# Two mixture-of-experts stages of a two-block kernel: float32r gathers and a smaller weight ring in the first, another order of the first expert's steps in the second

## The chip, the core and the metric

The kernel runs as one program on one core of a Trainium2 chip. The metric is the device time of one execution in microseconds (us). PE is TensorE, which multiplies matrices into PSUM banks (128 partitions x 512 f32 values). DVE (VectorE) and ACT (ScalarE) do elementwise work and carry results from PSUM to SBUF. SP issues the DMA transfers that bring weights from HBM.

## The reference

Two transformer-like blocks run one after the other on 256 tokens of width 1024, all in f32. Each has a token mixer and then a mixture of 32 experts. Only the mixtures matter here. The first picks two of eight experts within the best of four groups; the second picks four of 32 and has biases and a clipped activation:

```python
# first: eid = the two best experts of the best group, w = their weights; E = 32
def expert_block(args):                       # w_gate, w_up: 1024 x 256, w_down: 256 x 1024
    xb, e = args
    return (jax.nn.silu(xb @ w_gate[e]) * (xb @ w_up[e])) @ w_down[e]
# second: top_e = the four best experts, top_w = softmax of their logits
def expert_block(args):                       # w_gu: 1024 x 2048, w_dn: 1024 x 1024
    xe, e = args
    gu = xe @ w_gu[e] + b_gu[e]
    x_glu = jnp.minimum(gu[:, :D_FF], SWIGLU_LIMIT)
    x_lin = jnp.clip(gu[:, D_FF:], -SWIGLU_LIMIT, SWIGLU_LIMIT)
    act = (x_lin + 1) * (x_glu * jax.nn.sigmoid(SWIGLU_ALPHA * x_glu))
    return act @ w_dn[e] + b_dn[e]
# both: every token's results are summed with their weights
```

## The kernel before

**The weight ring.** Nearly all time after the first third of the kernel goes with 2 MB pieces of weights. The class `Ring` (lines 98 to 145) loads them in one fixed order through SP's queue (line 132). A piece is loaded into whichever buffer comes free next, so its transfer waits until the last matmul on the piece that lay there before, and every later piece queues behind it. In the first mixture the ring has four buffers of `ringp`, one more of the same pool under the tag `x`, NR1 = 3 of `ringq`, and one of `ringt` that serves until the first context product: nine buffers, then eight. In the second mixture it has seven.

**The first mixture** (lines 1575 to 1885) takes the 32 experts in eight quads of four, with 32 slots an expert. For quad q, `gather1` makes a 0/1 matrix `Sm` (token against slot) times the tokens' `rstd`, and multiplies it with `x1` on PE (line 1645) into the transposed inputs `xT`; `Sw` holds the same with the tokens' weights and goes through a transpose to `sT`. `up1` (line 1670) multiplies four pieces of gate and up weights, `act1` applies silu, `turn1` transposes, `down1` (line 1697) multiplies two pieces of down weights and adds into `acc` through `sT` (line 1706, the scatter). Slots above 32 are extra work under a branch that reads `nx1`; the trace shows it taken in quads 0 and 7. In quad q the gather of quad q+1 stands between `up1` and `turn1`. Ahead of quads 2, 3 and 4 stand three products of the context (lines 691 and 695), which belong to the second block and use ring pieces too. In quad 0, `weights1` (lines 1578 to 1586) and `extra_blocks1` (to line 1597, which makes `nx1`) run on DVE beside `up1`.

**The second mixture** (lines 2320 to 2840) starts with expert 0, whose weights (`gu` 0 and `dn` 0) are loaded early. `gather2_0` gathers its 64 slots (line 2508) and calls three steps: `compare` and `by_tokens`, which rank the experts by their number of tokens and open the ring for the rest, and `first2`, which issues `up2` (line 2566). Then `rest_by_rank` prepares weights, slots and biases (lines 2443 and 2451 pick the biases on PE) of the experts in ranked order, `gather2` gathers the next two items (line 2531, in float32r from `xh` and `xl`, where `xh` is the rounded value and `xl` the rest), and `down2` (line 2657) finishes expert 0. Items of four slim experts follow with `up2s` (line 2600) and `down2s` (line 2632).

A scheduler moves instructions within an engine's stream, so the order of the code is only roughly that of the engines.

Of the kernel before, what the change touches and what calls it, by code (L numbers as in the profile page):

```python
# [25 lines left out]
NR1 = 3  # L26
# [131 lines left out]
def _body(tc, nc, a, off, es, stop, dump):  # L158
# [11 lines left out]
    def trps():  # L170
        return ps("tr", 2)
# [1453 lines left out]

    def gather1(q, slots, tag, sT=None, between=None):

        Sm = pw1.tile([P, 2, 4, 32], F32, tag="Sm", name="Sm")
        Sw = pw1.tile([P, 2, 4, 32], F32, tag="Sw", name="Sw")
# [6 lines left out]
        xT = pw1.tile([P, 8, P], F32, tag="xT" + tag, name="xT")  # L1639
        for c2 in range(2):  # L1640
            pt = mmps() if tag else ps("sc", 2)
            for cc in range(4):
                c = 4 * c2 + cc
                for n in range(2):
                    PE.matmul(pt[:, P * cc:P * cc + P], xv1[:, n, c, :], Sm[:, n].rearrange("p e s -> p (e s)"),  # L1645
                              start=(n == 0), stop=(n == 1))
            for cc in range(4):
                c = 4 * c2 + cc
                if cc % 2:
                    S.activation(xT[:, c], pt[:, P * cc:P * cc + P], AF.Identity, scale=A2[:, c:c + 1], bias=sh2[:, c])  # L1650
                else:
                    V.tensor_scalar(xT[:, c], pt[:, P * cc:P * cc + P], A2[:, c:c + 1], sh2[:, c], op0=ALU.mult, op1=ALU.add)
        if between is not None:
            between(xT)
            for n in range(2):
                V.tensor_tensor(Sw[:, n], Sw[:, n], bcast(W1[:, n, e4, None], [P, 4, 32]), op=ALU.mult)
        pt = trps()
        for n in range(2):
            PE.transpose(pt[:, P * n:P * n + P], Sw[:, n].rearrange("p e s -> p (e s)"), ident)
        if sT is None:  # L1660
            sT = pw1.tile([P, 2, P], F32, tag="sT", bufs=2, name="sT")
        S.copy(sT, pt[:, :T].rearrange("p (c s) -> p c s", c=2))
        return xT, sT
# [12 lines left out]
    def act1(pg, tag):  # L1676
        act = pw1.tile([P, 256], F32, tag="act" + tag, name="act")
# [36 lines left out]
    def first1(xT):  # L1714
        pg.append(up1(0, xT, ""))
        weights1()
        extra_blocks1()

    nxt = gather1(0, iota[:, 0:32], "", between=first1)
# [112 lines left out]
    for q in range(8):  # L1832
# [17 lines left out]
        xT, sT = nxt  # L1850
# [11 lines left out]
        act = act1(up1(q, xT, "", True) if q else pg[0], "")  # L1862
        if q == 0:
# [558 lines left out]
    def rest_by_rank():  # L2422
        for n in range(2):
            chosen(n, ordr, M2)
        cnt = slots_of(M2, posm2)
        V.tensor_tensor(key, cnt, cap2, op=ALU.subtract)
        weights2(ordr)
        V.tensor_reduce(key[0:1, 0:1], key[0:1], axis=AX.X, op=ALU.max)
        V.tensor_scalar(over2, key[0:1, 0:1], 0.0, None, op0=ALU.max)

# [50 lines left out]
    def back2(Sw, w):  # L2481

        pt = trps()
        for n in range(2):
            PE.transpose(pt[:w, P * n:P * n + P], Sw[:, n, 0:w], ident)
        wc = pw2.tile([P, 1], F32, tag="wc2", bufs=3, name="wc2")
# [5 lines left out]
    def gather2_0(steps):  # L2492
# [22 lines left out]
        return xT, back2(Sw, 64)  # L2515
# [40 lines left out]
    def up2(r, xT, release=True):  # L2556
# [4 lines left out]
        for c in list(range(8)) + [-1] * (r == 0):  # L2561
            w = None if c < 0 else ring.get(("gu", r, c // 2)).rearrange("p (c f) -> p c f", c=2)[:, c % 2]
            for i in range(2):
                for j in range(2):
                    q, o = 4 * r + 2 * i + j, 1024 * i + 512 * j
                    PE.matmul(pg[i][64 * j:64 * j + 64, :], bcast(ident[:, q:q + 1], [P, 64]) if c < 0 else xT[:, c, :],  # L2566
                              bgu if c < 0 else w[:, o:o + 512], start=(r == 0 and c == 0), stop=(c == (7 if r else -1)),
                              tile_position=(0, 64 * j))
# [186 lines left out]
    xT, back = gather2_0((compare, by_tokens, first2))  # L2755
    ordered.close()
    rest_by_rank()
    r2.close()

# [105 lines left out]
```

## Time and profile before

| | before |
|---|---|
| median of three runs | 2023.31 us (2017.72 to 2023.66) |
| profiled execution | 2020.87 us, its span 2019.1 us |
| mean granted TensorE clock | 0.930 of full speed |
| PE busy | 1728.3 us, 86% of the span |
| DVE, ACT busy | 859.4 us (43%), 545.9 us (27%) |
| weight transfers through SP's queue | 628.04 MB, 79.9% of 16 DMA engines' span |

The span is the time from the first to the last instruction; the execution is 1.8 us longer. Busy shares are means over stages that have different limits, so the rows further down are by stage. A granted clock of 1.0 is TensorE's upper level (2.4 GHz), 0.5 its lower one (1.2 GHz).

### The profile page before, as it was taken

How to read it: one execution, taken by the hardware profiler on the slowest of the kernel's cores; microseconds unless marked ns; L12 is line 12 of the kernel's file. 1: busy time of each engine (PE TensorE's matmuls, PEld its weight loads, DVE VectorE, ACT ScalarE, POOL GpSimd, SP SyncE). 2: the span in 40 equal slices, each digit the busy share in tenths (PEclk: the TensorE clock that was granted, in tenths of full speed). 3: DMA queues.
4: the chain of work that ended last, by engine and by line, in shares of the span. 5: the costliest groups of instructions: out<-in, count | busy, mean ns of one | idle time of the engine just before them, and what ended most of it. 6: DMA issues, size and time to landing. Idle time of an engine off the chain costs nothing. (4 is left out here: it accounts for less than half of the span.)

```text
span 2019.1 us, 25531 instructions
## 1 busy us (share of the span) xinstructions
PE 1728.3 (86%) x10043; PEld 956.1 (47%) x10043; DVE 859.4 (43%) x1832; ACT 545.9 (27%) x1184; POOL 257.6 (13%) x232
## 2 busy tenths in 40 slices
PE   5899888989898878789999699886899988999855
PEld 2767667865554538578854133322233333333211
DVE  6998888553112248986644022211122222122112
ACT  4442566322011135566422011110021111111001
POOL 2576322200000005520100000000000000000000
PEclk8898899989999998899979799998899999999986
DMA  8624337976899986742457999999999999899996
GB/s 261 238 95 159 124 135 230 303 270 240 303 364 399 394 275 223 253 126 89 167 210 319 420 419 420 420 422 423 415 424 420 419 423 420 338 421 419 425 420 250
DMA packets 172666, 630.82 MB, mean 312 GB/s; under 512 B 25424, under 2 KB 32016, under 8 KB 152048
## 3 DMA queue, kind: packets, MB, share of 16 engines
q1 hardware_dynamic: 172112, 628.04, 79.9%
q8 instruction: 89, 1.46, 0.3%
q10 hardware_dynamic: 288, 0.52, 0.1%
q0 software_dynamic: 128, 0.39, 0.1%
q14 instruction: 49, 0.40, 0.1%
HBM read 627.88 MB, written 1.05 MB: 311 GB/s over the span
## 5 line engine op out<-in xcount | busy, mean ns | idle before, releaser
L2566 PE MATMUL mm<-w,xT 128*64 128x512 f32 x1472 | 332.0, 605 | 0.0
L2566 PEld LDWEIGHTS mm<-w,xT 128*64 128x64 f32 x1472 | 103.4, 139 | 205.2 <-issue 199.9
L2657 PE MATMUL o<-w,aT 128*64 128x512 f32 x640 | 149.6, 603 | 3.0 <-DMA w<-in_w_dn 3.0
L2600 PE MATMUL mm<-w,xT 128*32 128x512 f32 x768 | 106.6, 686 | 39.5 <-DMA w<-in_w_gu 39.5
L2575 DVE TENSOR_SCALAR g<-mm 128x512 f32<-128x512 f32 x23 | 15.9, 691 | 262.6 <-PE mm L2566 262.6
L2834 POOL TENSOR_TENSOR fin<-acc,fin 128x512 f32<-128x512 f32 x1 | 1.3, 1272 | 978.3 <-DVE acc L2832 978.3
L722 DVE TENSOR_TENSOR lo<-w,hi 128x512 fp32r<-128x512 f32 x126 | 102.1, 823 | 26.5 <-ACT hi L721 24.6
L709 PE MATMUL mm<-hTh,scratch 128*128 128x256 f32 x392 | 93.4, 315 | 9.6 <-DVE scratch L722 9.6
L721 ACT CAST hi<-w 128x512 fp32r<-128x512 f32 x126 | 76.7, 620 | 56.6 <-PE mm L709 50.0
L2632 PE MATMUL o<-w,aT 128*32 128x512 f32 x384 | 70.9, 780 | 23.0 <-DMA w<-in_w_dn 21.1
L2577 ACT ACTIVATE s<-g 128x512 f32<-128x512 f32 x23 | 14.5, 632 | 274.4 <-DVE g L2575 274.4
L2657 PEld LDWEIGHTS o<-w,aT 128*64 128x64 f32 x640 | 44.8, 138 | 87.3 <-issue 79.8
L709 PEld LDWEIGHTS mm<-hTh,scratch 128*128 128x128 f32 x392 | 71.6, 208 | 20.4 <-DVE scratch L722 9.2
L2672 DVE SCALAR_TENSOR_TENSOR yl<-yy,wc,yh 128x512 fp32r<-128x512 f32 (+1 forms) x30 | 21.4, 749 | 134.2 <-ACT yh L2671 134.0
L1670 PE MATMUL mm<-w,xT 128*32 128x512 f32 x640 | 72.0, 594 | 7.4 <-DVEq L1856 2.7
L2600 PEld LDWEIGHTS mm<-w,xT 128*32 128x32 f32 x768 | 23.1, 117 | 108.2 <-DMA w<-in_w_gu 62.1
L709 PE MATMUL mm<-hT3h,lo 128*128 128x256 f32 x192 | 61.4, 320 | 8.5 <-DVE lo L722 5.9
L2687 DVE TENSOR_TENSOR acc<-acc,sc 128x512 f32<-128x512 f32 x56 | 37.0, 685 | 68.3 <-PE sc L2679 68.3
L2662 ACT COPY yy<-o 64x512 f32<-64x512 f32 x40 | 23.2, 580 | 157.0 <-PE o L2657 156.6
L1645 PEld LDWEIGHTS sc<-Sm,x 128*128 128x128 f32 x256 | 61.6, 335 | 6.6 <-issue 5.0
L709 PE MATMUL mm<-scratch 128*128 128x256 f32 x216 | 64.7, 299 | 0.0
L1645 PE MATMUL sc<-Sm,x 128*128 128x128 f32 x256 | 63.2, 409 | 1.3 <-DVE Sm L1636 1.2
(706 smaller groups left out, 3462.2 us busy)
## 6 DMA issues: line engine op xcount, KB each, us to landing
w<-in_w_gu SPq DMA_DIRECT2D x128, 2048.0 KB, 19.9
w<-in_w_dn SPq DMA_DIRECT2D x63, 2048.0 KB, 23.0
w<-in_w_in SPq DMA_DIRECT2D x20, 2048.0 KB, 9.5
w<-in_moe_w_gate SPq DMA_DIRECT2D x32, 1024.0 KB, 10.8
w<-in_moe_w_up SPq DMA_DIRECT2D x32, 1024.0 KB, 12.8
w<-in_moe_w_down SPq DMA_DIRECT2D x32, 1024.0 KB, 13.8
w<-in_ada_w SPq DMA_DIRECT2D x12, 2048.0 KB, 9.7
w<-in_w_mod SPq DMA_DIRECT2D x12, 2048.0 KB, 8.8
```

What stands on the lines that cost most here:

```text
L709: PE.matmul(out, x, y, start=start and i == 0, stop=stop and i == 2)
L721: S.copy(hi, src)
L722: return parts, lambda: V.tensor_tensor(lo, src, hi.bitcast(F32), op=ALU.subtract)
L1645: PE.matmul(pt[:, P * cc:P * cc + P], xv1[:, n, c, :], Sm[:, n].rearrange("p e s -> p (e s)"), start=(n == 0), stop=(n == 1))
L1670: PE.matmul(pg[32 * j:32 * j + 32, :].rearrange("p (j f) -> p j f", j=2), xT[:, c, 32 * j:32 * j + 32], w[:, c % 2], start=(c == 0), stop= ...
L2566: PE.matmul(pg[i][64 * j:64 * j + 64, :], bcast(ident[:, q:q + 1], [P, 64]) if c < 0 else xT[:, c, :], bgu if c < 0 else w[:, o:o + 512], ...
L2600: PE.matmul(pg[32 * t:32 * t + 32, :], xT[:, c, :], w[:, 512 * ij:512 * ij + 512], start=False, stop=(c == 7), tile_position=(0, 32 * t))
L2632: PE.matmul(pd[32 * t:32 * t + 32, :], aT[:, f % 4, 2 * (1 - e) + f // 4, :], w[:, 512 * j:512 * j + 512], start=False, stop=(f == 7), til ...
L2657: PE.matmul(pd[64 * j:64 * j + 64, :], aT[:, f % 4, f // 4, :], w[:, 512 * j:512 * j + 512], start=False, stop=(f == 7), tile_position=(0, ...
L2662: S.copy(y[:, 512 * j:512 * j + 512], pd[64 * j:64 * j + 64, :])
L2672: V.scalar_tensor_tensor(yl[:, o], y[:, o], back[1], yh[:, o].bitcast(F32), op0=ALU.mult, op1=ALU.subtract)
L2687: V.tensor_tensor(o, o, pc, op=ALU.add)
```

## The change

In the first mixture the gathers of quads 1 to 7 are made two quads at a time in float32r: `normalised1` splits the normalised tokens into `xh1` and `xl1` (two instructions on ACT and two on DVE, 128 x 1024 each), and `gather1s` multiplies both with one `Sms` of 256 slots, in quads 0 (for 1 and 2), 2 (for 3 and 4), 4 (for 5 and 6) and 6 (for 7 alone, given twice). Quad 0's own gather and those of the extra slots stay as they were. NR1 becomes 2, so the ring has eight buffers and later seven. In the second mixture `gather2_0` uses two banks with `by_tokens` between their halves, `up2` of expert 0 begins with its bias rows and no longer ends with them, ACT's table for the sigmoid is loaded ahead, and expert 0's `down2` is written ahead of the picking of biases and of `gather2`.

```diff
-NR1 = 3
+NR1 = 2
...
+    def normalised1():
+        for n in range(2):
+            S.activation(xh1[:, n], xv1[:, n], AF.Identity, scale=rstd2[:, n:n + 1])
+            V.scalar_tensor_tensor(xl1[:, n], xv1[:, n], rstd2[:, n:n + 1], xh1[:, n].bitcast(F32), op0=ALU.mult, op1=ALU.subtract)
+
+    def gather1s(qs):
...
+        for c0 in range(0, 8, 2):
+            pt = ps("sc", 2)
+            for c in range(2):
+                for n in range(2):
+                    for x in (xl1, xh1):
+                        PE.matmul(pt[:, T * c:T * c + T], x[:, n, c0 + c, :], Sm[:, n], start=(n == 0 and x is xl1), stop=(n == 1 and x is xh1))
...
     def first1(xT):
         pg.append(up1(0, xT, ""))
+        normalised1()
         weights1()
         extra_blocks1()
...
         if q == 0:
+            turn1(act, aT)
             extras()
             ring.done(4)
-        if q < 7:
-            nxt = gather1(q + 1, iota[:, 0:32], "")
-        aT = pw1.tile([P, 2, P], F32, tag="aT", name="aT")
-        turn1(act, aT)
+        if q % 2 == 0:
+            _, backs1 = gather1s((q + 1, min(q + 2, 7)))
+        if q:
+            turn1(act, aT)
+        if q % 2 == 0:
+            quads = backs1()
         if q < 7:
             down1(q, aT, sT, q == 0, "")
...
-        pt = ps("sc", 2)
+        pts = [ps("sc", 2) for _ in range(2)]
+        for h in range(2):
+            for c in range(4):
+                for n in range(2):
+                    PE.matmul(pts[h][:, 64 * c:64 * c + 64], xv[:, n, 4 * h + c, :], Sm[:, n, 0:64], start=(n == 0), stop=(n == 1))
+            if h == 0:
+                steps[1]()
         for c in range(8):
-            for n in range(2):
-                PE.matmul(pt[:, 64 * c:64 * c + 64], xv[:, n, c, :], Sm[:, n, 0:64], start=(n == 0), stop=(n == 1))
-        steps[1]()
-        for c in range(8):
-            modulated(xT[:, c], pt[:, 64 * c:64 * c + 64], c)
+            modulated(xT[:, c], pts[c // 4][:, 64 * (c % 4):64 * (c % 4) + 64], c)
...
-        for c in list(range(8)) + [-1] * (r == 0):
+        for c in [-1] * (r == 0) + list(range(8)):
...
+        S.activation(warm, warm, AF.Sigmoid)
...
+    pt0 = turned2(Sw0, 64, ps("sc", 2))
     l = act2(pg)
+    slots_by_rank()
+    pd0 = bias2(0, xps())
+    aT0 = turn2(l, pw2.tile([P, 512], F32, tag="g2", name="aT0"))
+    back = back2(Sw0, 64, pt0)
+    down2(0, pd0, aT0, y)
+    ordered.close()
+    biases_by_rank()
+    r2.close()
     cur = gather2(pairs2[0])
-    down2(0, bias2(0, xps()), turn2(l, pw2.tile([P, 512], F32, tag="g2", name="aT0")), y)
```

What this does to the engines' order shows at three places. PE's stream in quad 1 of the first mixture, before: the four pieces of `up1`, the gather of quad 2 (L1645), the transposes of `Sw` and of `act`, then `down1`.

```order
L1670 MATMUL mm<-w_4158,xT 32x512 x8
L1670 MATMUL mm<-w_4161,xT 32x512 x8
L1670 MATMUL mm<-w_4287,xT 32x512 x8
L1670 MATMUL mm<-w_4384,xT 32x512 x8
L1645 MATMUL sc<-Sm,x_68 128x128 x16
L1659 MATMUL tr<-C,Sw 128x128 x2
L1686 MATMUL tr<-C,act 128x128 x2
L1697 MATMUL mm<-w_4387,aT 32x512 x2
L1697 MATMUL mm<-w_4390,aT 32x512 x2
```

The same place now:

```order
L1718 MATMUL mm<-w_4158,xTs 32x512 x8
L1718 MATMUL mm<-w_4290,xTs 32x512 x8
L1718 MATMUL mm<-w_4392,xTs 32x512 x8
L1718 MATMUL mm<-w_4395,xTs 32x512 x8
L1734 MATMUL tr<-C,act 128x128 x2
L1745 MATMUL mm<-w_4398,aT 32x512 x2
L1745 MATMUL mm<-w_4401,aT 32x512 x2
```

In the odd quads nothing stands between `up1` and `down1` but the transpose of `act`; in quads 0, 2, 4 and 6 there are 32 matmuls of 128 x 256 (L1649) and two pairs of transposes.

DVE's stream in quad 0, at the end of quad 0's own gather, before: `xT` is evicted and `weights1` begins.

```order
L1652 TENSOR_SCALAR xT<-sc,A_134,sh_132 128x128 x4
L1578 TENSOR_SCALAR gsc_4088<-t_4085 128x1
L1580 TENSOR_TENSOR gsc_4088<-t8b_4097 128x1
L1582 SCALAR_TENSOR_TENSOR gsc_4088<-gsc_4088 128x1
L1583 RECIPROCAL gsc_4088<-gsc_4088 128x1
```

The same place now:

```order
L1700 TENSOR_SCALAR xT<-sc,A_134,sh_132 128x128 x4
L1633 SCALAR_TENSOR_TENSOR xl_4171<-x_68,rstd_3796,xh_4170 128x1024 x2
L1578 TENSOR_SCALAR gsc_4088<-t_4085 128x1
L1580 TENSOR_TENSOR gsc_4088<-t8b_4097 128x1
L1582 SCALAR_TENSOR_TENSOR gsc_4088<-gsc_4088 128x1
```

The two `xl1` instructions stand ahead of all of `weights1`; ACT's two `xh1` stand likewise ahead of its part of `weights1`.

PE's stream in the second mixture, before, from the last piece of expert 0's `up2` on: bias rows, transposes of `Sw`, counts (L1489 to L1492), the picked biases and the next gather.

```order
L2566 MATMUL mm<-w_9264,xT_9518 64x512 x8
L2566 MATMUL mm<-bgu,C 64x512 x4
L2485 MATMUL tr<-C,Sw_9507 64x128 x2
L1489 MATMUL tr<-M_9456,C 128x32
L1490 MATMUL tr<-M_9456,C 128x64
L1491 MATMUL tr<-M_9456,C 128x32
L1492 MATMUL tr<-M_9456,C 128x32
L2443 MATMUL tr<-bgu,pick 128x512
L2554 MATMUL mm<-bgl,sel 128x512
L2451 MATMUL tr<-bdn,pick 128x512
L2531 MATMUL sc<-Sm_9675,xl 128x256
```

Expert 0's `down2` (16 matmuls of L2657) comes there only after all 32 matmuls of that gather and after the first piece of the next item's `up2s`. The same place now:

```order
L2629 MATMUL mm<-w_9246,xT_9502 64x512 x8
L2540 MATMUL sc<-C,Sw_9491 64x128 x2
L1489 MATMUL tr<-M_9438,C 128x32
L1490 MATMUL tr<-M_9438,C 128x64
L1491 MATMUL tr<-M_9438,C 128x32
L1492 MATMUL tr<-M_9438,C 128x32
L2711 MATMUL o<-bdn,C 64x512 x2
L2650 MATMUL tr<-C,l_9624 128x128 x4
L2719 MATMUL o<-w_9284,aT_9641 64x512 x8
L2719 MATMUL o<-w_9410,aT_9641 64x512 x8
L2500 MATMUL tr<-bgu,pick 128x512
L2594 MATMUL sc<-Sm_9693,xl 128x256
```

`down2` (L2719) now stands ahead of the picked biases and of the gather, and the bias rows (L2629 on `bgu`) have gone to the front of `up2`, out of this piece. Outside the two mixtures the engines' streams hold the same work in the same order, but for a few weight pieces that change places in SP's queue because other buffers come free first.

## Rows read from the trace of the kernel before

**Rows 1.** Windows, first mixture: PE, PEld, DVE, ACT, POOL, clock, DMA share, GB/s

```profile
440.00:590.00 150.00, 137.00 (x742) 81.60 (x746) 39.93 (x121) 19.64 (x46) 0.00 (x0) 0.95 0.79 295
...
590.00:710.00 120.00, 106.24 (x622) 65.04 (x615) 32.43 (x77) 15.03 (x37) 1.40 (x2) 0.99 1.04 396
...
530.00:560.00 30.00, 26.93 (x146) 19.43 (x146) 1.79 (x8) 1.55 (x3) 0.00 (x0) 0.94 0.75 273
```

**Rows 2.** PE's timeline in the first mixture: start, duration, operation, count, idle before

```profile
499.00 3.89 PE L1706 MATMUL sc<-y,sTx 128*128 128x512 f32 x8
...
532.35 15.74 PE L691 MATMUL mm<-hcT,w 128*128 128x256 f32 x64 [3.11 <-PEq L1774]
...
555.81 7.88 PE L1645 MATMUL sc<-Sm,x 128*128 128x128 f32 x32
564.99 3.64 PE L1697 MATMUL mm<-w,aT 128*32 128x512 f32 x32 [0.85 <-ACT aT L1687]
...
573.46 13.11 PE L695 MATMUL mm<-w,hcT 128*128 128x512 f32 x30
...
692.67 3.64 PE L1697 MATMUL mm<-w,aT 128*32 128x512 f32 x32 [0.85 <-ACT aT L1687]
...
718.81 7.07 PE L1670 MATMUL mm<-w,xT 128*32 128x512 f32 x64
727.86 0.63 PE L1697 MATMUL mm<-w,aT 128*32 128x512 f32 x3 [0.52 <-ACT aT L1687]
```

**Rows 3.** DMA issues, windows 700.9:701.5, 1049:1050, 1059.4:1059.5, 1084.9:1085: KB, us to landing

```profile
w<-in_moe_w_down SPq DMA_DIRECT2D x1, 1024.0 KB, 17.4
...
w<-in_w_gu SPq DMA_DIRECT2D x1, 2048.0 KB, 7.1
...
w<-in_w_gu SPq DMA_DIRECT2D x1, 2048.0 KB, 12.3
...
w<-in_w_gu SPq DMA_DIRECT2D x1, 2048.0 KB, 14.8
```

**Rows 4.** Windows of the second mixture, columns as in rows 1

```profile
1020.00:1040.00 20.00, 16.71 (x65) 14.48 (x65) 7.90 (x35) 2.31 (x7) 1.85 (x7) 0.52 0.07 25
...
1071.80:1081.50 9.70, 9.70 (x61) 4.69 (x61) 5.06 (x16) 2.35 (x5) 0.00 (x0) 0.99 0.01 2
...
1110.00:1150.00 40.00, 25.22 (x134) 5.61 (x134) 4.14 (x6) 1.22 (x3) 0.00 (x0) 0.71 1.01 419
1150.00:1500.00 350.00, 301.56 (x1505) 102.17 (x1499) 72.50 (x130) 47.05 (x95) 0.00 (x0) 0.95 1.01 420
```

**Rows 5.** PE's timeline, start of the second mixture, columns as in rows 2

```profile
1032.65 7.88 PE L2508 MATMUL sc<-Sm,x 128*128 128x64 f32 x32
...
1042.92 16.48 PE L2566 MATMUL mm<-w,xT 128*64 128x512 f32 x64
1059.22 1.88 PE L2566 MATMUL mm<-bgu,C 128*64 128x512 f32 x8
...
1075.44 0.60 PE L2588 MATMUL tr<-C,l 128*128 128x128 f32 x4
...
1077.83 7.09 PE L2657 MATMUL o<-w,aT 128*64 128x512 f32 x32
```

**Rows 6.** PE's timeline, first and last float32r gather matmul of sixteen

```profile
1073.21 0.39 PE L2531 MATMUL sc<-Sm,xl 128*128 128x256 f32 x1
...
1075.11 0.28 PE L2531 MATMUL sc<-Sm,xh 128*128 128x256 f32 x1
```

**Rows 7.** ACT, DVE, PE timelines: the split into xh, xl; quad 0's branch

```profile
1045.73 4.24 ACT L2467 ACTIVATE xh<-x,r 128x1024 fp32r<-128x1024 f32 x2
...
1047.91 4.17 DVE L2468 SCALAR_TENSOR_TENSOR xl<-x,r,xh 128x1024 fp32r<-128x1024 f32 x2 [0.31 <-ACT xh L2467]
...
458.68 0.16 DVE L1596 TENSOR_SCALAR nx<-nx 1x8 int32<-1x8 int32 x1
...
462.22 7.86 PE L1645 MATMUL mm<-Sm,x 128*128 128x128 f32 x32
```

More of the change, by code (lines that the diff above doesn't have):

```diff
@@ new lines, in gather1s @@
+    def gather1s(qs):
+        Sm = pw1.tile([P, 2, T], F32R, tag="Sms", name="Sms")
+        for i in range(2):
+            e4 = slice(4 * qs[i], 4 * qs[i] + 4)
+            for n in range(2):
+                V.tensor_tensor(Sm[:, n, P * i:P * i + P].rearrange("p (e s) -> p e s", e=4), bcast(posm1[:, n, e4, None], [P, 4, 32]),
+                                bcast(iota[:, None, 0:32], [P, 4, 32]), op=ALU.is_equal)
+        xT = pw1.tile([P, 8, T], F32, tag="xT", name="xTs")
+        for c0 in range(0, 8, 2):
[4 more added lines that the diff above has]
+                        PE.matmul(pt[:, T * c:T * c + T], x[:, n, c0 + c, :], Sm[:, n], start=(n == 0 and x is xl1), stop=(n == 1 and x is xh1))
+            for c in (c0, c0 + 1):
+                i = pt[:, T * (c - c0):T * (c - c0) + T]
+                if c % 2:
+                    S.activation(xT[:, c], i, AF.Identity, scale=A2[:, c:c + 1], bias=sh2[:, c])
+                else:
+                    V.tensor_scalar(xT[:, c], i, A2[:, c:c + 1], sh2[:, c], op0=ALU.mult, op1=ALU.add)
+        return xT, lambda: back1s(qs, xT, Sm)
@@ new lines, in back1s @@
+    def back1s(qs, xT, Sm):
+        out = []
+        for i in range(1 if qs[0] == qs[1] else 2):
+            e4 = slice(4 * qs[i], 4 * qs[i] + 4)
+            Sw = pw1.tile([P, 2, 4, 32], F32, tag="act", name="Sw")
+            for n in range(2):
+                V.tensor_tensor(Sw[:, n], Sm[:, n, P * i:P * i + P].bitcast(F32).rearrange("p (e s) -> p e s", e=4),
+                                bcast(W1[:, n, e4, None], [P, 4, 32]), op=ALU.mult)
+            pt = trps()
+            for n in range(2):
+                PE.transpose(pt[:, P * n:P * n + P], Sw[:, n].rearrange("p e s -> p (e s)"), ident)
+            sT = pw1.tile([P, 2, P], F32, tag="sT", bufs=3, name="sT")
+            S.copy(sT, pt[:, :T].rearrange("p (c s) -> p c s", c=2))
+            out.append((xT[:, :, P * i:P * i + P], sT))
+        return out
@@ L1638, in gather1 @@
                 V.tensor_tensor(Sw[:, n], Sw[:, n], bcast(W1[:, n, e4, None], [P, 4, 32]), op=ALU.mult)
-        xT = pw1.tile([P, 8, P], F32, tag="xT" + tag, name="xT")
+        xT = pw1.tile([P, 8, T if not tag else P], F32, tag="xT" + tag, name="xT")[:, :, :P]
         for c2 in range(2):
@@ L1715, in first1 @@
         pg.append(up1(0, xT, ""))
+        normalised1()
         weights1()
         extra_blocks1()
-    nxt = gather1(0, iota[:, 0:32], "", between=first1)
+    quads = [gather1(0, iota[:, 0:32], "", between=first1)]
     ordered.close()
@@ L1849, in _body @@
             expand(fgc, fgb)
-        xT, sT = nxt
+        xT, sT = quads.pop(0)
         aTx = pw1.tile([P, 2, P], F32, tag="aTx", name="aTx")
@@ L2420, in by_tokens, with weights_by_rank, slots_by_rank, biases_by_rank @@
         ring.open()
-    def rest_by_rank():
+    def weights_by_rank():
         for n in range(2):
             chosen(n, ordr, M2)
+        weights2(ordr)
+    def slots_by_rank():
         cnt = slots_of(M2, posm2)
         V.tensor_tensor(key, cnt, cap2, op=ALU.subtract)
-        weights2(ordr)
         V.tensor_reduce(key[0:1, 0:1], key[0:1], axis=AX.X, op=ALU.max)
         V.tensor_scalar(over2, key[0:1, 0:1], 0.0, None, op0=ALU.max)
+    def biases_by_rank():
         def pick(m, q):
@@ L2479, in modulated, with turned2, back2 @@
             V.tensor_scalar(dst, src, A4[:, c:c + 1], sh4[:, c], op0=ALU.mult, op1=ALU.add)
-    def back2(Sw, w):
-        pt = trps()
+    def turned2(Sw, w, pt):
         for n in range(2):
             PE.transpose(pt[:w, P * n:P * n + P], Sw[:, n, 0:w], ident)
+        return pt
+    def back2(Sw, w, pt=None):
+        if pt is None:
+            pt = turned2(Sw, w, trps())
         wc = pw2.tile([P, 1], F32, tag="wc2", bufs=3, name="wc2")
@@ L2504, in gather2_0 @@
         xT = pw2.tile([P, 8, 64], F32, tag="xT2", name="xT2")
-        pt = ps("sc", 2)
-        for c in range(8):
-            for n in range(2):
-                PE.matmul(pt[:, 64 * c:64 * c + 64], xv[:, n, c, :], Sm[:, n, 0:64], start=(n == 0), stop=(n == 1))
-        steps[1]()
-        for c in range(8):
-            modulated(xT[:, c], pt[:, 64 * c:64 * c + 64], c)
+        pts = [ps("sc", 2) for _ in range(2)]
+        for h in range(2):
+            for c in range(4):
+                for n in range(2):
+                    PE.matmul(pts[h][:, 64 * c:64 * c + 64], xv[:, n, 4 * h + c, :], Sm[:, n, 0:64], start=(n == 0), stop=(n == 1))
+            if h == 0:
+                steps[1]()
+        for c in range(8):
+            modulated(xT[:, c], pts[c // 4][:, 64 * (c % 4):64 * (c % 4) + 64], c)
         steps[2](xT)
@@ L2566, in up2 @@
                     PE.matmul(pg[i][64 * j:64 * j + 64, :], bcast(ident[:, q:q + 1], [P, 64]) if c < 0 else xT[:, c, :],
-                              bgu if c < 0 else w[:, o:o + 512], start=(r == 0 and c == 0), stop=(c == (7 if r else -1)),
-                              tile_position=(0, 64 * j))
+                              bgu if c < 0 else w[:, o:o + 512], start=c < 0, stop=c == 7, tile_position=(0, 64 * j))
             if release and c % 2 and c > 0:
@@ L2753, in first2 @@
         normalised()
[L2755 to L2758, printed above, removed]
+        S.activation(warm, warm, AF.Sigmoid)
+    warm = pr.tile([P, 1], F32, name="warm")
+    V.memset(warm, 0.0)
+    xT, Sw0 = gather2_0((compare, by_tokens, first2))
+    weights_by_rank()
     def aT2():
```

13 lines of the change are left out of this document (8 added, 5 removed).

## The prediction

> **What bounds the kernel now.** The page's slices of transfer rate come first: they are flat near 420 GB/s through the whole second mixture and lower and uneven through the first. The windows split the first mixture in two. From 440 to 590 us the transfers move 295 GB/s; from 590 to 710 they move 396 and the engines' share is 1.04 [rows 1]. A 2 MB piece (2.097 MB) thus takes 5.30 us when the queue is full, and of the first 150 us 150 x (1 - 295/396) = 38 us are idle for transfers. So PE sets the pace up to 590 and the transfers are saturated from there to the last down piece, which is issued at 700.9 and lands 17.4 us later, at 718.3 [rows 3]. PE still doesn't wait for them at the end: quad 6's `down1` starts at 692.67, released by ACT's copy of `aT` [rows 2], while its second piece, six pieces ahead of the last, lands at 718.3 - 6 x 5.30 = 686.5.
>
> In the second mixture the windows show a hole and then a wall. The last piece that `up2` of expert 0 makes room for is issued at 1059.4 and lands 12.3 us later, at 1071.7 [rows 3]. From 1071.8 to 1081.5 the transfers are at 0.01 [rows 4], since every buffer is full and the next to come free are those of expert 0's down weights, which PE reads from 1077.83 on [rows 5]. From 1110 to the end of the streaming they are at 1.01, 420 GB/s [rows 4]; that is 4.99 us a piece at most. PE has idle time there (25.22 of 40 us busy from 1110 to 1150), so the order of PE's work is worth nothing later, and what the hole costs is carried to the end whole.
>
> **The change, first mixture.** Each old gather takes 7.88 us and stands, with its transposes and a wait of 0.85, between `up1` and `down1`: from 555.81 to 564.99, 9.2 us [rows 2]. Without a gather that stretch is what quad 7 shows, 718.81 + 7.07 to 727.86, 2.0 us. So quads 1, 3 and 5 lose 7.2 us each on PE. A float32r gather of two quads is 32 matmuls. The like ones (L2531) start (1075.11 - 1073.21)/15 = 0.127 us apart [rows 6]; 32 make 4.1, and with three pairs of transposes the stretch is about 5.6: quads 2, 4 and 6 lose 3.6 each. Its evictions lie beside it on ACT and DVE, which have little to do there, and its result is needed only a quad later.
>
> Quad 0 loses instead of gaining. The split costs 4.24 on ACT and 4.17 on DVE, DVE half of one behind ACT [rows 7], so DVE starts `weights1` some 6.3 us later. Behind `weights1` in DVE's stream stand `nx1`, made at 458.68, the product in `act1` and the extra slots' `Sm`; PE waits for all of these at the branch, and `turn1` now stands ahead of it too. The extra gather began at 462.22, 3.5 us after `nx1` [rows 7]. Bounds for its delay: 4.3 if only 1.5 of those 3.5 recur, 11 if the silu and the transposes come on top in full. I take 8.7, nearer to the second, because ACT's silu queues behind its own split and two copies. After it, the double gather saves 9.2 - 5.9 = 3.3. Quad 1 starts at 499.00 + 3.89 + 8.7 - 3.3 = 508.3 where it was 502.9.
>
> From there PE goes faster than the ring. Quad 1: 0.9 for the branch + 7.07 + 2.0 + 3.64 + 3.89 = 17.4, so quad 2 starts at 525.7. Quad 2: its context product 3.0 + 15.8 + 0.75 to the next start, then 7.07 + 5.6 + 3.64 + 3.89 = 39.6 altogether, so quad 3 starts at 565.3. Its own context product ends 14.1 later (13.11 and the way to it [rows 2]), at 579.4. With one buffer less, the buffer that this frees is the one that takes the last context piece (before, it took the piece behind that, the first of quad 4). A transfer that starts on an empty queue landed 7.1 us after its issue [rows 3]; with 0.9 for the issue, the piece lands at 587.4, and from there I expect the queue to stay full: the 24 pieces of quads 4 to 7 x 5.30 = 127.2 put the last down piece at 714.6, and quad 6's second down piece, six before it, at 682.8. PE waits for that one now. `down1` of quad 6 starts at 682.9 and not at 692.67: **9.8 us** earlier, and what follows is the same work as before. Bounds: the delay of quad 0 and the stretch of 5.6 (7 if each bank waits for its eviction) pass through to that landing, which gives 2 to 14. I take 9, as a transfer now and then starts late.
>
> **The change, second mixture.** Order first: `by_tokens` sits behind half of the 7.88 us gather [rows 5], so the first ranked piece is issued some 4 us earlier. That is worth nothing by itself, because the next pieces still wait for `up2` of expert 0. With its bias rows in front, at the lower clock (0.52 up to 1040 [rows 4]), `up2` frees its pieces about 1 us later than before, and its end comes at about 1060.2 where it was 1059.22 + 1.88 = 1061.1. Then min, sigmoid (its table already there), product, transposes and copy follow: an estimate of 4.4 for five steps of the size of the transposes' 0.60 [rows 5] with a handoff each, so `down2` starts at 1064.6 where it was 1077.83. It frees its first piece after half of 7.09, at 1068.1, the second at 1071.7. The queue is busy until about 1072.7, so these two pieces land at 1077.6 and 1082.5. The third waits for the first piece of the next item, which PE reads after the picked biases and the double gather: 4.1 + about 3 for the picks, 2.5 for biases and transposes, 1.9 for the piece and 1.2 of waits, 12.7 behind 1071.7, so 1084.4. Landing 7.1 later it is there at 1091.5; before, the third piece was issued at 1084.95 and took 14.8 [rows 3], 1099.75. **Gain 8.3 us.** Behind it the queue stays full, and the lead is kept to the end. Bounds: 9.7 if PE reads that piece 1.4 us sooner (two pieces), 3.3 if the picks and the gather run at the lower clock throughout, 5 us more.
>
> Sum: 9 + 8.3 = 17.3 from 2020.87 (the span of 2019.1 and 1.8 around it), 2003.6; the median shown is 2.4 us above that execution, its lowest run 3.2 below. I say **2004**, own range 1997 to 2011.
>
> **A rule against it.** From 1110 to 1150 PE waits for pieces and the granted clock is 0.71, where over the next 350 us, with PE busy 86%, it is 0.95 [rows 4]. 0.71 is a mixture of the two levels, 2.4 GHz (1.0) and 1.2 GHz (0.5). The forecast makes PE wait in quads 5 and 6, so quad 6's `down1` (3.64 [rows 2]) could run at the lower level and take twice that: 2003.6 + 3.6 = 2007, rival 1 below. The Trainium skill, "TensorE: Matmul & The Clock Gate", section "HAM oscillation — how this bites in real kernels", says that waits on transfers between bursts of matmuls throttle the clock again; by that rule the time is rival 1's, and the trace agrees in the 0.71 of that row. As for the transfers, the Trainium skill, "SBUF — State Buffer", section "Summary: rules for kernel authors", counts with about 358 GB/s from HBM; by it the two pieces of the hole would be worth 11.7 us, but this trace moves 420, and the measurement decides.
>
> **Rivals.**
> 1. *The clock falls in quad 6* (12 in 100): 2007. For it the 0.71 above; against it, the waits that I work out there are 1 to 4 us each, and from 590 to 710 the clock is 0.99 [rows 1].
> 2. *The first mixture gives nothing* (13): if quad 0's delay and the smaller ring together put the last context piece at 591.1 (718.3 - 127.2), the transfers end as before and only PE's slack of 6 us at quad 6 is there to win or lose. For it: 1.04 from 590 on. Against it: 38 us of idle transfer time ahead. 2020.87 - 8.3 = 2012.6, or less.
> 3. *The second mixture gives nothing* (8): the third piece waits as long as before, because the clock falls just when `down2` runs and everything behind it comes late. 2020.87 - 9 = 2011.9.
> 4. *The ring keeps up* (7): PE's savings come through whole, 3 x 7.2 + 3 x 3.6 - 5.4 = 27 us, with the 8.3: 1985.6. Against it: 24 pieces at 5.30 can't be passed.
> 5. *Slower* (5): the ring is what starves. From 530 to 560 the transfers fall to 0.75 because no buffer is free [rows 1], 7.5 us lost in 30; one buffer less could make a loss like it in each of quads 1 to 4, 30 us, and the first mixture would end 20 us later: about 2033. It decides if the last context piece lands after 587.4 + 17.3 = 604.7.
> 6. *Neither comes through* (5): rivals 2 and 3 at once, 2020.9.
>
> The forecast has 50 in 100. It and rivals 1 to 4 are faster by over 0.3% (6 us, about what a measurement of this kernel tells from no change): 90, of which I give 3 to cases that end short of 6. So 0.87, same 0.08, slower 0.05. The range 1995 to 2014 leaves out rivals 4 to 6, 17 in 100, and a rest of 3.
>
> **What would show it.** In the profile after: `weights1` and the extra gather of quad 0 later by 4 to 11 us; no f32 gather but quad 0's and the extras'; PE waits for gate, up and down pieces in quads 5 and 6; quad 6's `down1` near 683; the transfer share close to 1 between 1072 and 1084; the third piece after expert 0's near 1091. Wrong would be: the first mixture's transfers idle longer than 38 us, `down2` of expert 0 after 1070, or a hole of the same length moved behind it.

## The result and the profile after

The changed kernel takes **2001.53 us** (median of four runs, 2000.47 to 2002.98) where the kernel before took 2021.33 in the same series: a ratio of 0.990, 95% interval 0.9885 to 0.9916. The forecast was 2004, 1995 to 2014.

The profiled execution has a span of 2000.7 us, 18.4 less than before. Three anchors that both kernels share, all starts on PE, split the span: the first gather of the first mixture (445.12 before, 443.97 after), the first instruction of the stage behind that mixture (749.84 and 742.05), and the first gather of the second mixture (1032.65 and 1025.19).

| stretch | before | after | gain |
|---|---|---|---|
| up to the first mixture's first gather | 445.12 | 443.97 | 1.2, unchanged work |
| first mixture | 304.72 | 298.08 | 6.6 |
| stages between | 282.81 | 283.14 | -0.3 |
| second mixture's first gather to the end | 986.45 | 975.53 | 10.9 |

The first mixture by windows after the change, which answer to [rows 1]: PE, PEld, DVE, ACT and POOL busy, granted clock, DMA share, GB/s.

```profile
440.00:590.00 150.00, 129.75 (x754) 67.59 (x757) 41.27 (x105) 24.52 (x47) 0.00 (x0) 0.92 0.79 296
590.00:710.00 120.00, 97.05 (x572) 43.84 (x565) 30.06 (x67) 13.44 (x31) 1.40 (x2) 0.91 1.04 396
```

PE is busy 7.3 and 9.2 us less in the two stretches, and the transfers move no more than before: 296 GB/s against 295, then 396 in both. PE's own rows show where it now waits (start, duration, operation, count, idle before and what ended it):

```profile
469.64 7.88 PE L1693 MATMUL mm<-Sm,x 128*128 128x128 f32 x32 [0.88 <-DVE Sm L1684]
...
502.93 3.89 PE L1754 MATMUL sc<-y,sTx 128*128 128x512 f32 x8
...
561.53 3.89 PE L1754 MATMUL sc<-y,sT 128*128 128x512 f32 x8
...
609.25 8.77 PE L1718 MATMUL mm<-w,xTs 128*32 128x512 f32 x64 [0.96 <-PEq L1905]
...
675.17 3.58 PE L1718 MATMUL mm<-w,xTs 128*32 128x512 f32 x16 [3.46 <-DMA w<-in_moe_w_up]
...
685.09 3.62 PE L1745 MATMUL mm<-w,aT 128*32 128x512 f32 x26 [0.51 <-DMA w<-in_moe_w_down]
```

Quad 6's `down1` no longer waits for ACT's copy of `aT` [rows 2] but for its second down piece, which ends its wait at 685.09. Counted from the first gather that is 241.1 us; before, `down1` started at 692.67 - 445.12 = 247.6. The last down piece of the mixture is issued at 700.1 and takes 16.5:

```profile
w<-in_moe_w_down SPq DMA_DIRECT2D x1, 1024.0 KB, 16.5
```

So it lands at 716.6, 272.7 us after the first gather, and before at 718.3 [rows 3], 273.2 after it. Quad 6's second down piece is two transfers of 1 MB; the last of them, issued at 667.61 before and at 667.83 after, landed thus (before, then after):

```profile
w<-in_moe_w_down SPq DMA_DIRECT2D x1, 1024.0 KB, 17.5
```

```profile
w<-in_moe_w_down SPq DMA_DIRECT2D x1, 1024.0 KB, 17.2
```

So it was there 240.0 us after the first gather before, 7.5 us ahead of `down1`, and after the change at 241.1, just when `down1` goes on. **The transfers end where they ended; PE has caught up with them.**

Windows show from where on the queue is full. Before, it ran low in two stretches:

```profile
540.00:550.00 10.00, 9.28 (x50) 7.19 (x52) 1.29 (x6) 1.17 (x2) 0.00 (x0) 1.00 0.27 81
...
585.00:591.00 6.00, 5.28 (x40) 1.58 (x42) 1.29 (x6) 0.59 (x1) 0.00 (x0) 1.00 0.56 193
```

After, the windows from 505 to 590:

```profile
505.00:531.00 26.00, 20.13 (x117) 7.28 (x118) 6.56 (x10) 0.76 (x2) 0.00 (x0) 0.95 0.98 363
531.00:541.00 10.00, 10.00 (x46) 8.74 (x45) 0.00 (x0) 0.58 (x1) 0.00 (x0) 0.96 0.83 315
541.00:580.00 39.00, 37.58 (x189) 17.25 (x187) 8.43 (x19) 5.25 (x11) 0.00 (x0) 1.00 1.03 392
580.00:590.00 10.00, 8.26 (x74) 2.61 (x77) 0.42 (x1) 0.93 (x3) 0.00 (x0) 1.00 1.04 384
```

SP issues the first context piece here, and the last one, issued at 579.58, lands 9.0 us later:

```profile
503.02 0.56 SPq L132 DMA_DIRECT2D w<-in_w_in  x1
```

```profile
w<-in_w_in SPq DMA_DIRECT2D x1, 1024.0 KB, 9.0
```

After the change the queue is full from the first context piece on, which is issued at 503.02, when quad 0 has done with its down pieces. In these windows it runs low only once, at 531, while SP stands at the branch of line 1823 until its own transfers have landed. The last context piece is 1 MB and not 2; when it is issued, four down transfers are still on their way, and it lands at 588.6, 2.9 us behind the last of them. So PE's pace in quads 1 to 3 holds up no transfer any more, where before it did from 540 to 550 and from 585 to 591.

The delay in quad 0 shows on DVE and ACT, whose splits stand ahead of `weights1`:

```profile
455.96 4.20 DVE L1633 SCALAR_TENSOR_TENSOR xl<-x,rstd,xh 128x1024 fp32r<-128x1024 f32 x2 [2.62 <-ACT xh L1632]
460.09 0.14 DVE L1578 TENSOR_SCALAR gsc<-t 128x1 f32<-128x1 f32 x1
```

The extra gather starts at 469.64, 25.7 us after the first; before it was 462.22 - 445.12 = 17.1 [rows 7].

The second mixture, PE's timeline, which answers to [rows 5]:

```profile
1025.19 4.10 PE L2570 MATMUL sc<-Sm,x 128*128 128x64 f32 x16 [1.13 <-DVE Sm L2563]
1029.22 0.63 PE L2470 MATMUL tr<-sq,pcol 32*128 32x32 f32 x2
...
1033.77 3.50 PE L2629 MATMUL mm<-bgu,C 128*64 128x512 f32 x8
1037.11 13.90 PE L2629 MATMUL mm<-w,xT 128*64 128x512 f32 x64
...
1054.70 7.09 PE L2719 MATMUL o<-w,aT 128*64 128x512 f32 x32 [0.72 <-ACT aT L2651]
```

`down2` starts 29.5 us after the gather and not 45.2. The third piece behind expert 0's is issued at 1071.99 and lands 8.5 later:

```profile
w<-in_w_gu SPq DMA_DIRECT2D x1, 2048.0 KB, 8.5
```

That is 1080.5, 55.3 after the gather; before it was 1099.75 [rows 3], 67.1 after it. Of these 11.8 us 10.9 are left at the end. The windows show that the hole has gone, and something that was not forecast (before, then after, the same stretch counted from the gather; after, the stretch from 1063.9; columns as above):

```profile
1063.50:1071.90 8.40, 7.00 (x23) 4.82 (x22) 3.90 (x15) 3.65 (x5) 0.00 (x0) 0.60 0.79 337
```

```profile
1056.00:1064.40 8.40, 8.33 (x39) 3.29 (x35) 1.57 (x6) 2.52 (x5) 0.00 (x0) 1.00 1.01 424
...
1063.90:1073.60 9.70, 9.70 (x71) 5.32 (x74) 7.58 (x20) 4.05 (x8) 0.00 (x0) 1.00 0.90 358
```

The transfers are at 0.90 in a stretch like that in which they were at 0.01 [rows 4]. And the granted clock stays at its upper level, where before, in the sparse stretch of picks and waits behind `up2`, it was 0.60.

### The profile page after: what moved, and what is told of

It reads as the page before. It is cut to its first block, busy times and chain, and to the rows that moved or that the text cites. A ratio compares the mean times of both kernels' runs of the same rounds, so it can differ in the third digit from the quotient of the medians.

```text
span 2000.7 us, 25312 instructions
## 1 busy us (share of the span) xinstructions
PE 1697.7 (85%) x9947; PEld 917.9 (46%) x9947; DVE 857.9 (43%) x1811; ACT 548.1 (27%) x1175; POOL 257.8 (13%) x232
## 5 line engine op out<-in xcount | busy, mean ns | idle before, releaser
L2629 PE MATMUL mm<-w,xT 128*64 128x512 f32 x1472 | 329.7, 601 | 0.0
L2629 PEld LDWEIGHTS mm<-w,xT 128*64 128x64 f32 x1472 | 103.1, 138 | 202.8 <-issue 201.0
L2719 PE MATMUL o<-w,aT 128*64 128x512 f32 x640 | 150.7, 606 | 3.3 <-DMA w<-in_w_dn 2.6
L2662 PE MATMUL mm<-w,xT 128*32 128x512 f32 x768 | 103.1, 672 | 31.5 <-DMA w<-in_w_gu 31.5
L2719 PEld LDWEIGHTS o<-w,aT 128*64 128x64 f32 x640 | 45.0, 139 | 87.7 <-issue 80.3
L1718 PE MATMUL mm<-w,xTs 128*32 128x512 f32 x448 | 55.0, 635 | 17.3 <-DMA w<-in_moe_w_up 9.7
L709 PE MATMUL mm<-hT3l,hi 128*128 128x256 f32 x192 | 56.5, 294 | 0.2 <-DVE hT3l L705 0.2
L709 PE MATMUL mm<-hT3h,hi 128*128 128x256 f32 x192 | 56.2, 293 | 0.0
```

The source lines that it names most:

```text
L709: PE.matmul(out, x, y, start=start and i == 0, stop=stop and i == 2)
L1718: PE.matmul(pg[32 * j:32 * j + 32, :].rearrange("p (j f) -> p j f", j=2), xT[:, c, 32 * j:32 * j + 32], w[:, c % 2], start=(c == 0), stop= ...
L2662: PE.matmul(pg[32 * t:32 * t + 32, :], xT[:, c, :], w[:, 512 * ij:512 * ij + 512], start=False, stop=(c == 7), tile_position=(0, 32 * t))
L2719: PE.matmul(pd[64 * j:64 * j + 64, :], aT[:, f % 4, f // 4, :], w[:, 512 * j:512 * j + 512], start=False, stop=(f == 7), tile_position=(0, ...
```

## The experiments

The theory after the result: two separate gains. In the first mixture PE gains on the transfers until it meets them in quads 5 and 6; whatever reaches the last context piece earlier moves all that follows, and PE's work in quads 4 to 6 is worth nothing. In the second, `down2` frees the two buffers that the transfers wait for. By the traces the first of these needs a correction: the piece that counts is the first context piece, at the end of quad 0, and PE's pace behind it is worth nothing as long as the queue stays full. From its issue to the landing of quad 6's second down piece the change takes 182.0 us, and the eight kernels below that keep its float32r gathers 181.4 to 184.5, whether that issue comes 48.6 us after the first gather (extras in float32r), 52.6 (split early) or 59.0 (the change). In the table below the first column is from the first mixture's first gather to the stage behind it, the second from the second mixture's first gather to the end, both of the profiled execution; ratios are to the kernel before in the same series.

| kernel | first mixture | second | median | ratio, 95% interval |
|---|---|---|---|---|
| before | 304.7 | 986.5 | 2021 to 2022 | 1 |
| the change | 298.1 | 975.5 | 2001.53 | 0.990 (0.9885 to 0.9916) |
| first part only | 298.2 | 985.7 | 2016.01 | 0.9967 (0.9954 to 0.998) |
| second part only | 304.9 | 976.3 | 2010.79 | 0.9945 (0.9929 to 0.996) |
| before, ring of two | 305.0 | 986.2 | 2024.39 | 1.0007 (0.9995 to 1.002) |
| split early | 292.5 | 975.8 | 1997.48 | 0.987 (0.9851 to 0.9889) |
| `down2` late | 298.3 | 986.1 | 2013.78 | 0.9967 (0.9952 to 0.9982) |
| bias rows last | 298.0 | 976.5 | 2002.08 | 0.9897 (0.9881 to 0.9914) |
| ranking late | 300.2 | 976.8 | 2003.35 | 0.990 (0.9877 to 0.9923) |
| light gathers late | 297.4 | | 2001.73, one run | |
| extras in float32r | 286.0 | 976.7 | 1993.74 | 0.9861 (0.9841 to 0.9882) |
| the same, 128 columns | 292.3 | 976.0 | 1995.15 | 0.986 (0.9837 to 0.9883) |

**The first part only.** The hunks of the diff ahead of line 2000; the second mixture as before.

```diff
-NR1 = 3
+NR1 = 2
...
+        normalised1()
...
+        if q % 2 == 0:
+            _, backs1 = gather1s((q + 1, min(q + 2, 7)))
```

> Only the first mixture's part of the change (NR1 = 2, the split, the float32r gathers). In the profile of the whole change quad 6's down1 starts 241.1 us after the first gather, before it was 247.6. Theory (two separate gains that add): 6.4 us of gain here, some 2014 to 2015 beside 2021.3 for the kernel before, and the hole of the second mixture as it was before (transfers at 0.01 for 10 us behind expert 0's pieces). Rival (the first part only gives way to the second, which would take it back or need it): under 3 us here.

The first mixture takes 298.2 us, as in the whole change, and the hole of the second is there as before (granted clock 1.00, DMA share 0.00):

```profile
1066.80:1076.50 9.70, 9.70 (x60) 4.51 (x60) 4.68 (x16) 2.35 (x5) 0.00 (x0) 1.00 0.00 0
```

**The second part only.** The other hunks, on the kernel before.

```diff
+    down2(0, pd0, aT0, y)
+    ordered.close()
+    biases_by_rank()
+    r2.close()
     cur = gather2(pairs2[0])
-    down2(0, bias2(0, xps()), turn2(l, pw2.tile([P, 512], F32, tag="g2", name="aT0")), y)
```

> Only the second mixture's part of the change, with NR1 = 3 and the old gathers in the first. In the profile of the whole change the third piece behind expert 0's lands 55.3 us after the second mixture's first gather starts, before it was 67.2. Theory (the hole in the transfers is shortened and the lead is kept to the end): 11 to 12 us of gain, some 2010. Rival (the lead is lost further on, because PE becomes the bound): under 8 us, with PE waiting less for w_gu and w_dn from 1105 to 2019 than the 60.6 us of before.

10.2 us of the second stretch, a little under what was expected, and the first stretch is untouched. 0.9967 x 0.9945 = 0.9912, inside the interval of the whole change: within the noise the two parts add, and neither needs the other.

**The ring of two.**

```diff
-NR1 = 3
+NR1 = 2
```

> The kernel before with NR1 = 2 and nothing else. Theory (following the pieces buffer by buffer, the old gathers leave PE so slow up to 590 us that one buffer less costs nothing): same time within 2 us. Rival (the ring starves, one more loss like that from 530 to 560 in each of the quads 1 to 4): 10 us or more slower, quad 6's down1 later than 247.6 us behind the first gather by as much.

305.0 against 304.7 and a ratio whose interval takes in 1: a buffer less costs the old gathers nothing that can be measured. The rival that foresaw a starving ring falls. What the smaller ring costs the new gathers, no run shows.

**The split early.** `normalised1` moves from `first1` to the point behind quad 0's `Sm`, where DVE and ACT wait for PE's gather.

```diff
-    def gather1(q, slots, tag, sT=None, between=None):
+    def gather1(q, slots, tag, sT=None, between=None, early=None):
...
+        if early is not None:
+            early()
         xT = pw1.tile([P, 8, T if not tag else P], F32, tag="xT" + tag, name="xT")[:, :, :P]
...
         pg.append(up1(0, xT, ""))
-        normalised1()
         weights1()
...
-    quads = [gather1(0, iota[:, 0:32], "", between=first1)]
+    quads = [gather1(0, iota[:, 0:32], "", between=first1, early=normalised1)]
```

> The whole change, with the split into xh1 and xl1 moved ahead of the evictions of quad 0's gather, while DVE and ACT wait for that gather, instead of ahead of weights1. Theory (quad 0's delay of 8.6 us passes through PE's chain to the last context piece, and from it through the full queue to quad 6's down1): the extra gather of quad 0 starts about 17.5 us after the first gather and not 25.7, and the whole is 6 to 8 us shorter than the change, some 1994 to 1996. Rival (the transfers are full anyway from earlier on and swallow it): within 2 us of 2001.5.

Quad 0's delay goes through to the end, though not quite whole. PE's timeline of this kernel, its extra gather, and quad 6's `down1`:

```profile
464.06 2.14 PE L1695 MATMUL mm<-Sm,x 128*128 128x128 f32 x8 [0.88 <-DVE Sm L1684]
...
680.36 3.62 PE L1747 MATMUL mm<-w,aT 128*32 128x512 f32 x26 [0.59 <-DMA w<-in_moe_w_down]
```

The extra gather starts 464.06 - 444.74 = 19.3 us after the first, 6.4 sooner than in the change, and quad 6's `down1` has its second piece 235.6 after it, 5.5 sooner. The 17.5 that was expected for the first number was wrong by 1.8: the split is out of the way (`nx1` is made 13.6 us after the first gather, as before the change), so the rest probably lies with `turn1` ahead of the branch, which was not undone by itself. The rival's premise, that the transfers are full from earlier on, is right, but the delay lies ahead of that: the first context piece too is issued 6.4 us sooner. The medians differ by 4.1 us, less than the 6 to 8 expected; the two kernels ran in different series, whose kernels before differ by 1.0.

**`down2` late.** The change with the old place of expert 0's second product.

```diff
-    pd0 = bias2(0, xps())
-    aT0 = turn2(l, pw2.tile([P, 512], F32, tag="g2", name="aT0"))
     back = back2(Sw0, 64, pt0)
-    down2(0, pd0, aT0, y)
     ordered.close()
     biases_by_rank()
     r2.close()
     cur = gather2(pairs2[0])
+    down2(0, bias2(0, xps()), turn2(l, pw2.tile([P, 512], F32, tag="g2", name="aT0")), y)
```

> The whole change, with expert 0's down2 written behind the picked biases and gather2 again, as before; bias rows first, two banks and the early table as in the change. Theory (the gain of the second mixture is the place of down2, since its two buffers are the next to come free): nearly all of the 11.9 us is lost, the third piece behind expert 0's lands 64 to 66 us after the first gather, time 2009 to 2013. Rival (the earlier clock and the shorter up2 give it): 2002 to 2005.

986.1: the second mixture's gain is gone as a whole, and the hole is back:

```profile
1066.90:1072.60 5.70, 5.70 (x31) 1.73 (x31) 2.04 (x9) 1.04 (x2) 0.00 (x0) 1.00 0.00 0
```

The third piece lands 66.0 us after the gather, within the 64 to 66 expected. The place of `down2` is the cause; bias rows, banks and the early table give nothing without it. The median, 2013.78, lies 0.8 above what was expected.

**Bias rows last.**

```diff
-        for c in [-1] * (r == 0) + list(range(8)):
+        for c in list(range(8)) + [-1] * (r == 0):
...
-                              bgu if c < 0 else w[:, o:o + 512], start=c < 0, stop=c == 7, tile_position=(0, 64 * j))
+                              bgu if c < 0 else w[:, o:o + 512], start=(r == 0 and c == 0), stop=(c == (7 if r else -1)), tile_position=(0, 64 * j))
```

> The whole change, with the bias rows of expert 0's up2 at its end again. Theory (the rows at the front run at the lower clock while nothing else could, and take 1.9 us off the way from the last piece to down2): down2 starts 1 to 2 us later, the third piece behind expert 0's too, time 2002 to 2004. Rival (no difference, since PE's work is the same): 2001.5 within 0.7.

The first piece of `down2` is free 35.4 us after the gather and not 33.2, the third piece lands 57.5 after it and not 55.3, and 1.0 us of that is left at the end. `down2` itself starts only 0.5 us later than in the change, not 1 to 2. In time the two theories can't be told apart, since the medians differ by 0.6. In this profile the clock falls just behind `up2`, with the first part of `down2` in it, which takes 8.71 us and not 7.09:

```profile
1057.60:1061.60 4.00, 3.96 (x12) 1.27 (x14) 1.52 (x7) 0.00 (x0) 0.00 (x0) 0.58 1.02 428
```

The same fall stands in two profiles with the bias rows first (ranking late; extras in float32r), and there too the first piece of `down2` is free only 35.5 and 35.4 us after the gather. So most of this loss is the clock's, and that the bias rows' place is worth anything is not shown.

**Ranking late.**

```diff
-            if h == 0:
-                steps[1]()
+        steps[1]()
         for c in range(8):
```

> The whole change, with the ranking of the experts behind both halves of the first gather of the second mixture. Theory (the first ranked piece is issued 4 us later, but the pieces behind it wait for up2's releases): same time, 2001.5 within 1.5. Rival (that first piece is on the path): 4 us slower, 2005.

The second stretch is 1.3 us longer, in a profile with the clock's fall just told of; the median is 0.3 above what was expected, the ratio that of the change: the earlier issue of the first ranked piece is worth little or nothing, as was said. (The 300.2 in the first mixture is of this execution; its code there is that of the change. In it the transfers took 184.5 us from the first context piece to quad 6's second down piece.)

**Light gathers late.** Quads 4 and 6 make a quarter of their gather. This leaves out work that quads 5 to 7 need, so only the times of the first mixture are read.

```diff
+                if qs[0] in (5, 7):
+                    PE.matmul(pt[:, T * c:T * c + T], xh1[:, 0, c0 + c, :], Sm[:, 0], start=True, stop=True)
+                    continue
                 for n in range(2):
```

> The whole change, but the gathers that stand in quads 4 and 6 make only 8 of their 32 matmuls (xh1 of the first 128 tokens alone), so that quads 5 to 7 compute with other inputs; what comes behind the first mixture is not compared. Theory (from the last context piece on the transfers set the pace): quad 6's down1 starts 241.1 us after the first gather as in the change, within 1.5, and PE only waits longer for its pieces. Rival (PE's own work sets the pace): 3 us earlier for quad 4's gather, 238.

Quad 6's `down1` waits for its second piece until 685.88 - 445.42 = 240.5 after the first gather, 0.7 sooner than in the change and not 3:

```profile
685.88 3.62 PE L1748 MATMUL mm<-w,aT 128*32 128x512 f32 x26 [1.47 <-DMA w<-in_moe_w_down]
```

PE's work in quad 4's gather has no price; the wait takes its place.

**Extra slots in float32r.** On the kernel of the early split, the last f32 gathers behind quad 0's own become float32r too.

```diff
+    def gatherx(q, sT):
+        Sm = pw1.tile([P, 2, T], F32R, tag="Sms", name="Smx")
...
+                    for x in (xl1, xh1):
+                        PE.matmul(pt[:, T * c:T * c + T], x[:, n, c0 + c, :], Sm[:, n], start=(n == 0 and x is xl1), stop=(n == 1 and x is xh1))
...
-                turn1(act1(up1(q, gather1(q, iota[:, 32:64], "x", sTx)[0], "x"), "x"), aTx)
+                turn1(act1(up1(q, gatherx(q, sTx), "x"), "x"), aTx)
```

> The change with the early split (the kernel of the split moved ahead), and the extra slots' gathers of quads 0 and 7 in float32r too, with 256 columns of which 128 are doubles. Theory (all that PE saves in quad 0 passes through to quad 6's down1, and all that it saves in quad 7, behind the last piece, to the end): the extra gather takes about 4.1 us and not 7.9, the last scatter of the first mixture ends 6 to 8 us sooner than with the early split alone (286.9 after the first gather), 279 to 281, time 1990 to 1992. Rival (transfers swallow quad 0's part): 283, 1993 to 1994.

The first mixture is 6.5 us shorter than with the early split, within the 6 to 8. Quad 6's second down piece lands 5.4 us sooner after the first gather than there, and the end of quad 7 gains the rest. The median, 1993.74 us, is the lowest here, 0.9861 of the kernel before; but 1990 to 1992 was expected, it lies where the rival had it, and its ratio can't be told from that of the early split (0.987). So this gain is shown by the profiles and not by the medians. Its matmuls stand 0.12 us apart at the upper clock:

```profile
463.82 0.28 PE L1734 MATMUL mm<-Smx,xh 128*128 128x256 f32 x1
463.94 0.28 PE L1734 MATMUL mm<-Smx,xl 128*128 128x256 f32 x1
...
467.40 0.28 PE L1734 MATMUL mm<-Smx,xh 128*128 128x256 f32 x1
```

**The same with 128 columns.** In `gatherx` `T` becomes `P`, without doubles.

```diff
-                        PE.matmul(pt[:, T * c:T * c + T], x[:, n, c0 + c, :], Sm[:, n], start=(n == 0 and x is xl1), stop=(n == 1 and x is xh1))
+                        PE.matmul(pt[:, P * c:P * c + P], x[:, n, c0 + c, :], Sm[:, n], start=(n == 0 and x is xl1), stop=(n == 1 and x is xh1))
```

> As the one before, with 128 columns and no doubles in the extra gathers. If a float32r matmul of 128 columns costs half of one of 256 (0.127 us), the extra gather takes 2 us and the last scatter ends 2 us or more sooner than there in each of two quads; if it costs as much or more than one of 256, the doubles are free and this kernel is no faster.

Half the columns save next to nothing: 0.11 us from one to the next, as long as the clock is up. In this execution it falls in the middle of the gather, though PE is busy throughout, and the first mixture takes 6.3 us more than with doubles; the timed runs don't show that difference (0.986 and 0.9861), so how often it falls stays open.

```profile
464.99 0.28 PE L1734 MATMUL mm<-Smx,xh 128*128 128x128 f32 x1
465.10 0.28 PE L1734 MATMUL mm<-Smx,xl 128*128 128x128 f32 x1
```

```profile
465.00:469.00 4.00, 4.00 (x23) 4.00 (x24) 0.77 (x3) 1.02 (x3) 0.00 (x0) 0.59 0.42 155
```

## Why the prediction was right, and which terms were off

**Quad 0's delay: right.** 8.7 forecast, 25.7 - 17.1 = 8.6 measured. That it is the split and that it goes through to the end was shown by moving the split: 6.4 sooner at the extra gather, 5.5 at quad 6.

**The chain to the last context piece: its time nearly right, its reason wrong.** Quad 1 was to start 508.3 - 445.1 = 63.2 us after the first gather; it did at 62.9. Quad 3: 120.2 forecast, 561.53 + 3.89 - 443.97 = 121.5 measured. The last context piece was to land at 142.3; it was issued at 579.6 and took 9.0 where the forecast allowed 8, and landed at 144.6. But the step "a transfer that starts on an empty queue" does not hold for it. Its 7.1 us are of a 2 MB piece [rows 3], and this one is 1 MB; and the queue had been full since the first context piece, but for the branch at 531, and the last piece landed when the four transfers ahead of it were through. That the time came within 2.3 us is luck. By the traces, what the forecast worked out for quads 1 to 3 bears on PE's waits and no longer on the end; only quad 0's part does. No run changes quads 1 to 3 alone. (That quad 1 by itself adds up to 17.5 and not 17.4, and quad 2 to 39.8 and not 39.6, changes little.)

**The gain of the transfers: mis-sized.** The step "24 pieces x 5.30 put the last down piece at 714.6" gave the transfers a lead of 718.3 - 714.6 = 3.7 us. They had 0.5: 272.7 against 273.2 after the first gather. Of the 3.2 missing, 2.3 come from that landing and 0.8 from the queue, which took 128.0 us for the 24 pieces and not 127.2. At quad 6's second down piece there was no lead at all: the forecast had it at 686.5 before, by 5.30 a piece counted back from the end, but it landed at 685.1, 240.0 us after the first gather, and after the change at 241.1. So the whole gain is the other summand of the 9.8, PE's slack: before, `down1` of quad 6 started 7.5 us after its piece was there, and now it goes on when it lands. 7.5 - 1.1 = 6.4, and 6.6 at the end of the mixture, where 9 was said. That is the picture of rival 2, which had the transfers ending as before and called the slack of 6 us something to win or lose; it gave 2012.6 "or less", no gain in the first mixture and an open rest, and that rest was 6.6.

**The ring.** Rival 5 (it starves) is refuted by the result and, for the old gathers, by the ring of two; rival 4 (it keeps up) by the result and by the light gathers: PE's work in quad 4's gather has no price.

**The second mixture's hole: right in place and kind, short by 2.6.** Without the new place of `down2` nothing of the gain is left, as its undoing showed. 8.3 was forecast, the third piece came 11.8 sooner and 10.9 stayed. Two steps were too long. `down2` was to start 32.0 us after the gather and did at 29.5; 1.7 of that is `up2`, which ran at the upper clock nearly throughout (13.90 us, before 16.48 [rows 5]), the rest the steps between them. And from the end of `down2` to the end of the next item's first piece the forecast had 12.7, the trace 1071.98 - 1061.79 = 10.2, in which PE never waited and the clock was at 1.00; the gather had been priced at that level, so it is the steps around it and the waits that were priced too long. Against these 4.9, the third piece took 8.5 to land and not 7.1. Nothing of the clock was foreseen but as a loss.

**The clock rule.** Rival 1 had the clock fall in quad 6. It fell: 0.91 from 590 to 710, before 0.99. Quad 4's `up1` took 8.77 and not 7.07, behind waits of 0.91 and 2.64 us for DVE, and the last quarter of quad 6's, behind a wait of 3.46, took 3.58, where a quarter of the 7.07 of [rows 2] is 1.8. The Trainium skill, "TensorE: Matmul & The Clock Gate", section "HAM oscillation — how this bites in real kernels", says that waits for transfers throttle the clock again, and the trace agrees in quad 6's 3.58 behind that wait; quad 4's fall stood behind waits for DVE. It cost nothing in quad 6, because PE waited for the next piece anyway and `down1` ran at the upper level again (3.62).

**Both errors together.** 2.4 too much in the first mixture, 2.6 too little in the second, and 1.2 us that the profiled execution gained ahead of both: so the sum came within 2.5 us of the median by terms that were each off by more than a quarter of what was forecast. That closeness is luck.

## What to carry to other kernels

Where PE and the transfers take turns as the bound, follow each buffer: an edit is worth what it moves the one piece from which the queue stays full, and PE's savings behind that piece only turn into waits. Which piece that is, the landings tell, and not PE's chain. What a stream of pieces waits for is the release of a buffer, so the step that frees the next one belongs ahead of all preparation that frees none. A preparation that is needed late (here the split for the next gathers) belongs where its engines wait, not ahead of the chain that a branch waits for.

## What the runs showed of the hardware

A float32r matmul of 128 columns costs nearly as much here as one of 256, 0.11 and 0.12 us from start to start at the upper clock. So an f32 gather of 128 columns (7.88 us) becomes 4.1 us in float32r with its columns doubled, and by an estimate of 32 x 0.11 still 3.5 without. In the one profile with 128 columns the granted clock fell to 0.59 while PE was busy all the time (4.00 of 4 us), where with 256 columns it stayed at 1.00; whether the narrower matmuls are the cause was not repeated. The sparse stretch of picks and small transposes behind `up2` took the clock from 1.00 to 0.60 in the kernel before, and it fell there in all four profiles with that order. With `down2` in its place it stayed up in the profile of the change and in four others; in three (bias rows last, ranking late, extras in float32r) it fell for 3.4 us all the same, so that place does not rule the fall out.
